# A decoder layer's front: feature-major rows, two native first chunks, the row scale entering at their sums

## The chip, the cores and the metric

The kernel runs on one core of one Trainium2 chip, in one launch. The metric is the time of the core in device microseconds (us); lower is better. Engines are named as in the profile: PE (TensorE matmul), PEld (its weight load), DVE (VectorE), ACT (ScalarE), POOL (GpSimd), SP (SyncE, which here only issues DMAs).

## The reference, cut to what matters

One layer of a hybrid decoder over 256 positions of width 1,024, in float32:

```
n = RMSNorm(x) * norm_mix_g
z = n @ w_in              # c_a, c_g, q, k, v, qi, ki, wi, gate logits
u = c_a * sigmoid(c_g)    # 1024 channels
u = causal depthwise conv of u, 31 taps, + conv_b
y_conv = silu(LayerNorm(u)) @ w_conv_out
y_attn = DSA(q, k, v, qi, ki, wi) @ w_attn_out       # top 64 of the keys by an index score
h = x + (g_conv * y_conv + g_attn * y_attn) @ w_mix_out
h = h + CrossAttn(RMSNorm(h), RMSNorm(mem))          # 256 memory rows
h = h + relu(RMSNorm(h) @ w_ff1)^2 @ w_ff2
out = RMSNorm(h)
```

RMSNorm divides a row by the root of its mean square, so the divisor (here `rstd`, one number for each of the 256 positions) is a factor of the whole row, while the gain `norm_mix_g` belongs to the 1,024 features. A product with the weights can therefore be taken before the row's factor is known, and the factor put to the result.

## The kernel before

**Layout and stream.** Activations lie feature-major: 8 tiles (`kt`) of 128 features by 256 positions. All weights come through one stream of chunks (`STREAM`, L34 to L53), in the order in which PE uses them: four `conv` chunks, `qi`, `ki`, four more `conv`, `gc`, `ga`, `v`, `q` and `k`, `xk`, `xv`, `ao`, `co`, `mix` and so on. A chunk is 1 MB, [128 x 2,048] float32, and holds two output tiles ("halves") of 8 `kt` each. For `conv` the first half is the gate, the second the value. Three buffers (`raws`) hold the raw chunks; a few (`EARLY`) lie elsewhere. `load` issues the DMA of the next chunk from SP, and is called when a chunk's last half has been split.

**Two ways to multiply.** Ordinarily each half of weights is split into a high part (ACT, L178) and a low part (DVE, the `lo` of L181), both in the form fp32r, and so are the activations (`n2`). A tile is then three products for each `kt`, 24 matmuls (`tile_b`). A chunk in `WHOLE` is instead multiplied in native float32, unsplit: 8 matmuls for a tile, each of which the profile lists as two records. Before, `conv` 0 and `co` 0 are in `WHOLE`.

**The front (L321 to L410).** Two DMAs bring x row-major (`x_rm`). ACT squares and sums each row (`row_square`), DVE and POOL make `rstd`, DVE scales the rows, PE transposes them, ACT and DVE take them out of PSUM times the gain (`n_f`), then split them into `n2`. Ten matmuls of zeros (`ps_warm`) run ahead on PE. `vec`, the gains and biases, comes by a DMA that POOL issues (L325).

**The convolution.** `conv_in` (L471) makes `u` of one channel tile. Its 31 taps run one instruction each: the first on ACT, the other 30 on DVE, as jobs in a list `fill`. When all eight tiles have had their taps, `layer_norm` (L595) is started as a generator. Its steps go one at each call of `tick`: reserve a tile; mean on PE (`ps_mub`), subtraction, squares, sums; the last sums (`vs`); the square root (`ps_vr`, POOL's power `rs_vr`); the spread (`ps_rsb`), the product with it and Silu on `acc`, after which `normed` is set; then the split of `acc` into `u2` in four steps. Ahead of the `co` chunks the program drains `fill` and calls `tick` until `normed` is set (L705 to L708). `co` 0 multiplies `acc` itself in native float32; `co` 1 to 3 use `u2`.

**Who goes when.** The program is written in one order, by hand, and each engine executes its part of it in order. What DVE does between PE's tiles is dealt out while the program is written, by a planner with prices of its own, which are numbers in the code and not measurements. `pe.total` grows by 2,560 for a tile of 24 matmuls. `dve.total` grows by elements / 0.96 + 70 (125 with a scalar from a pointer): 1,137 for a `lo`, 337 for a product of 256, 391 down to 360 for a tap as its length falls from 255 to 226. `tick`, called after each tile, steps the generators and then hands out taps:

```
        while (len(fill) > 1 or (fill and (len(done) > 5 or nused[0] < 5))) and dve.total < pe.total - 1000:
            fill_one()
        dve.total = max(dve.total, pe.total - 2000)
```

Each use of weights also calls `split_ahead` (L213), which puts one `lo` on DVE and one high part on ACT for halves that come later. Both totals are set to zero at the end of the front (L410).

Of the kernel before, what the change touches and what calls it, by code (L numbers as in the profile page):

```python
# [8 lines left out]
F32 = mybir.dt.float32  # L9
# [3 lines left out]
ALU = mybir.AluOpType  # L13
# [42 lines left out]
N_CHUNK = KT * S  # L56
HALVES = 6
EARLY = (3, STREAM.index(("co", 0)))
WHOLE = (("conv", 0), ("co", 0))


class Counted:
# [49 lines left out]
def block_kernel(ctx, tc, x, xt, mem, memt, wst, wki, vecs, convw, gout, out):  # L112
# [30 lines left out]
    def ps_acc(name):  # L143
        return bank("acc", 4, name)
# [9 lines left out]
    def load(parts=1):  # L154
        if nload[0] >= len(STREAM):
            return
        c = nload[0]
        nload[0] += 1
        key = STREAM[c]
        raw = t8(f"raw{c}", F32, (P, N_CHUNK)) if c in EARLY else raws.tile([P, N_CHUNK], F32, tag="raw", name=f"raw{c}")  # L160
        n = KT * NK if key[0] == "ki" else N_CHUNK
        src = wki if key[0] == "ki" else wst[INDEX[key]]
        for q in range(parts):
            ns = slice(q * n // parts, (q + 1) * n // parts)
            nc.sync.dma_start(raw[:, ns], src[:, ns])
        if key in WHOLE:
            whole[key] = raw.rearrange("p (k n) -> p k n", k=2 * KT)
            return
        parts = 1 if key[0] == "ki" else 2
        for q in range(parts):  # L170
            ns = slice(q * n // parts, (q + 1) * n // parts)
            high_jobs.append(lambda ns=ns, q=q, last=q == parts - 1: high(key, c, raw, ns, q, last))
# [82 lines left out]
    def tile_b(ps, w, x2, kts=range(KT), wide=False):  # L255


        ps = ps[: w[0].shape[2]]
        for kt in kts:
            wh, wl = w[0][:, kt, :], w[1][:, kt, :]  # L260
            if not wide:
                mm_b(ps[:, :S], wh, wl, x2, kt, kt == 0, kt == KT - 1)
            elif kt == 0:
                pe.matmul(ps, wh, x2.both(kt), start=True, stop=False)
                pe.matmul(ps[:, S:], wl, x2.high(kt), start=False, stop=False)
            else:
                pe.matmul(ps[:, S:], wl, x2.high(kt), start=False, stop=False)
                pe.matmul(ps, wh, x2.both(kt), start=False, stop=kt == KT - 1)
# [49 lines left out]
        return lambda ct, ps: act(dst[:, ct, :], ps, AF.Copy)  # L318


    x_rm = t8("x_rm", F32, (P, 2, D))  # L321
    for rb in range(2):
        nc.sync.dma_start(x_rm[:, rb, :], x[rb * P : (rb + 1) * P, :])
    vec = cst.tile([P, 72], F32, name="vec")
    nc.gpsimd.dma_start(vec, vecs)  # L325
    bgc, bga, cvb, lng, lnb, g_mix, g_mem, g_x, g_ffn = (vec[:, 8 * j : 8 * j + 8] for j in range(9))
    cw = cst.tile([P, KT, TAPS], F32, name="cw")
    for parts in (2, 2, 1):
        load(parts)
    nc.sync.dma_start(cw, convw.rearrange("p (k t) -> p k t", k=KT))  # L330
    load()
    zero = w2("zero")
    nc.vector.memset(zero, 0.0)
# [12 lines left out]
    nc.scalar.activation(half, half, AF.Sigmoid, bias=0.0, scale=0.0)  # L346
    nc.gpsimd.memset(half, -0.5)
    ps = ps_aux("ps_warm")
    for j in range(10):
        nc.tensor.matmul(ps, zero_r[:, :P], zero_r, start=True, stop=True)  # L350


# [5 lines left out]
    def row_square(src, rb, ss):  # L358
        junk = w2(f"junk_{src.name if hasattr(src, 'name') else ''}{rb}", BF16, (P, D))
        act(junk, src[:, rb, :], AF.Square, accum_out=ss[:, rb : rb + 1])  # L360

    def rsqrt(sums, name):

        ps = ps_aux(f"ps_{name}")
        for rb in range(2):
            pe.matmul(ps[:, 2 * rb : 2 * rb + 2], sums[:, rb * P : rb * P + P], onesd[:, :2], start=True, stop=True)
        ms = small.tile([P, 2], F32, tag="ms", name=f"ms_{name}")
        dve.tensor_scalar(ms, ps[:, :4].rearrange("p (r t) -> p r t", r=2)[:, :, 0], EPS, None, ALU.add)
        return power(ms, name)
# [12 lines left out]


    n2 = parts_t8("n_p")
    n_f = t8("n_f")
    ss = small.tile([P, 2], F32, tag="ss", name="ss_n")
    ptn = [ps_acc(f"pt_n{c}") for c in range(4)]
    for rb in range(2):
        row_square(x_rm, rb, ss)
    for rb in range(2):  # L390
        ms = small.tile([P, 1], F32, tag="ms1", name=f"ms_n{rb}")
        dve.tensor_scalar(ms, ss[:, rb : rb + 1], 1.0 / D, EPS, ALU.mult, ALU.add)
        rs = small.tile([P, 1], F32, tag="rs1", name=f"rs_n{rb}")
        nc.gpsimd.tensor_tensor(out=rs, in0=ms, in1=half[:, 0:1], op=ALU.pow)
        dve.tensor_scalar(x_rm[:, rb, :], x_rm[:, rb, :], rs[:, 0:1], None, ALU.mult)
        for kt in range(KT):
            pe.transpose(ptn[kt // 2][:, (kt % 2) * S + rb * P : (kt % 2) * S + rb * P + P],
                         x_rm[:, rb, kt * P : kt * P + P], ident)
    for kt in range(KT):
        src = ptn[kt // 2][:, (kt % 2) * S : (kt % 2) * S + S]  # L400
        if kt % 2 == 1:
            dve.tensor_scalar(n_f[:, kt, :], src, g_mix[:, kt : kt + 1], None, ALU.mult)
        else:
            act(n_f[:, kt, :], src, AF.Copy, scale=g_mix[:, kt : kt + 1])
    for c in range(0, KT, 2):
        split(n2.high(c, 2), n2.low(c, 2), n_f[:, c : c + 2, :])
    split_high()
    split_low()
    split_high()
    pe.total = dve.total = 0.0  # L410


    mem2 = parts_t8("mem_p")
# [3 lines left out]
    def memory():  # L417
        mem_rm = t8("mem_rm", F32, (P, 2, D))
        mem_t = t8("mem_t")
        nc.sync.dma_start(mem_rm, mem.rearrange("(r p) d -> p r d", p=P))  # L420
        nc.sync.dma_start(mem_t, memt)
        yield
        yield
        yield
        ss = small.tile([P, 2], F32, tag="ss", name="ss_m")
        for rb in range(2):
            row_square(mem_rm, rb, ss)
            yield
        dve.tensor_scalar(ss, ss, 1.0 / D, EPS, ALU.mult, ALU.add)
        nc.gpsimd.tensor_tensor(out=rs_m, in0=ss, in1=half, op=ALU.pow)  # L430
# [26 lines left out]
        return go  # L457

    def conv_tile(i, half):
        key = ("conv", i)  # L460
        w = weights("conv", i, half, KT) if key not in WHOLE else None
        split_ahead()
        ps = ps_mm(f"ps_conv{i}{half}")
        if w:
            tile_b(ps, w, n2)
        else:
            for kt in range(KT):
                pe.matmul(ps[:, :S], whole[key][:, half * KT + kt, :], n_f[:, kt, :], start=kt == 0, stop=kt == KT - 1)
        return ps

    def conv_in(i):  # L471
        psg = conv_tile(i, 0)
        sg = w2(f"sg{i}", F32, (P, S))
        act(sg, psg[:, :S], AF.Sigmoid)
        tick()
        psa = conv_tile(i, 1)
        dve.tensor_tensor(out=u[:, i, :], in0=psa[:, :S], in1=sg, op=ALU.mult)
        tick()
        tap(i, 0)()
        fill.append([tap(i, s) for s in range(1, TAPS)])  # L480
        if ("conv", i) in WHOLE:
            load()

    for i in range(4):
        conv_in(i)
        if i == 1:
            start(memory())


    qi_t = t8("qi_t", F32, (P, 4, S))  # L490
# [635 lines left out]
```

## Time and profile before

| | |
|---|---|
| median of 3 runs | 516.89 us (516.72 to 516.94) |
| the profiled execution: its own time | 516.86 us |
| its span, first to last instruction | 515.1 us |
| mean granted TensorE clock | 0.998 |
| busy: PE, PEld, DVE, ACT, POOL | 98%, 90%, 81%, 56%, 4% |
| DMA | 92.75 MB, mean 180 GB/s |

The span is 1.76 us shorter than the execution's own time; that remainder is taken as fixed. PE's busy share says that the matmuls follow each other, not that each is as fast as it could be. In a timeline row the two numbers ahead are the start and the length of a merged group, `xN` is its count of instructions, and the brackets hold the idle time ahead of it and who ended it.

### The profile page before, as it was taken

Reading aid. Unit: us, or ns where it says so; the run is one execution under the profiler, and the core shown is the slowest. Engines: PE = TensorE matmul, PEld = TensorE weight load, DVE = VectorE, ACT = ScalarE, POOL = GpSimd, SP = SyncE. Lnnn points to the kernel's source line nnn. Section 1 sums busy time; section 2 is a strip of 40 time slices with the busy share of each in tenths; the row PEclk is TensorE's granted clock in tenths of the full one; section 3 lists DMA queues with packets and bytes.
Section 4 is the critical chain, followed back from the end, with each engine's and each line's share of the span. In section 5 each row is a group of like instructions: output and inputs, shape, how many; then the busy total and the mean of one; then the engine's idle time right before and its main releaser. Section 6 shows DMA issues by size and latency. Waiting matters only on the chain.

```text
span 515.1 us, 8515 instructions
## 1 busy us (share of the span) xinstructions
PE 504.3 (98%) x3354; PEld 463.1 (90%) x3354; DVE 419.4 (81%) x796; ACT 286.9 (56%) x489; POOL 19.2 (4%) x30
## 2 busy tenths in 40 slices
PE   7999999999999999999999999999999999999995
PEld 5999999999899999999999998988888888888884
DVE  4998999999988999999898976696766566666565
ACT  5666655546446666656655657565654454554442
POOL 2000000001001000021000000000000000000000
PEclk9999999999999999999999999999999999999999
DMA  8856435464552343454744541446445554445402
GB/s 317 359 187 236 155 122 205 174 225 183 194 216 102 144 164 118 155 224 161 275 143 155 207 184 44 181 165 242 164 169 220 221 207 163 164 174 219 181 1 81
DMA packets 14311, 92.75 MB, mean 180 GB/s; under 512 B 1584, under 2 KB 2480, under 8 KB 3776
## 3 DMA queue, kind: packets, MB, share of 16 engines
q1 hardware_dynamic: 13952, 91.85, 48.3%
q8 instruction: 26, 0.43, 0.3%
q10 hardware_dynamic: 288, 0.33, 0.2%
q14 instruction: 13, 0.11, 0.1%
q0 software_dynamic: 32, 0.04, 0.0%
HBM read 91.16 MB, written 1.05 MB: 179 GB/s over the span
## 4 chain that ended last, share of the span: by engine, by line
PE 95%; issue 1%; ACT 1%; DVE 1%; DMA 1%; POOL 0%; POOLq 0%; DVEq 0%; ACTq 0%
PE ps_f L77 17%; PE ps_ff L77 16%; PE ps_conv L77 9%; PE ps_co L77 5%; PE ps_ao L77 4%; PE ps_ga L77 4%; PE ps_gc L77 4%; PE ps_k L77 4%; PE ps_q L77 4%; PE ps_mix L77 4%; PE ps_v L77 4%; PE ps_xo L77 3%; PE ps_xq L77 2%; PE ps_qi L77 2%; PE ps_xk L77 2%; PE ps_xv L77 2%
## 5 line engine op out<-in xcount | busy, mean ns | idle before, releaser
L77 DVE TENSOR_TENSOR lo<-raw,hi 128x1024 fp32r<-128x1024 f32 x161 | 195.7, 1225 | 3.3 <-ACT hi L178 1.6
L178 ACT ACTIVATE hi<-raw 128x1024 fp32r<-128x1024 f32 x161 | 166.4, 1047 | 2.5 <-PE ps_v L77 2.5
L77 DVE SCALAR_TENSOR_TENSOR acc<-u,cw,acc 128x255 f32<-128x255 f32 (+27 forms) x240 | 100.6, 475 | 0.6
L77 PE MATMUL ps_f<-ff_p,hi 128*128 128x512 f32 x256 | 89.8, 396 | 0.0
L77 PE MATMUL ps_ff<-hi,fs 128*128 128x512 f32 (+1 forms) x256 | 80.8, 387 | 0.0
L77 PE MATMUL ps_f<-ff_p,lo 128*128 128x256 f32 x256 | 66.2, 279 | 0.0
L77 PEld LDWEIGHTS ps_ff<-hi,fs 128*128 128x128 f32 x256 | 47.9, 188 | 9.2
L77 PEld LDWEIGHTS ps_f<-ff_p,hi 128*128 128x128 f32 x256 | 46.8, 188 | 9.2
L77 DVE TENSOR_TENSOR ft<-ps_f,ft 128x256 f32<-128x256 f32 x32 | 13.6, 423 | 46.4 <-ACT ft L957 46.4
L77 PEld LDWEIGHTS ps_f<-ff_p,lo 128*128 128x128 f32 x256 | 48.2, 188 | 2.6
L957 ACT ACTIVATE ft<-ps_f 128x256 f32<-128x256 f32 x32 | 12.2, 380 | 66.9 <-PE ps_f L77 66.9
L77 PE MATMUL ps_ff<-lo,fs 128*128 128x512 f32 (+1 forms) x128 | 49.4, 386 | 0.0
L77 PE MATMUL ps_conv<-n_p,hi 128*128 128x256 f32 x224 | 41.0, 285 | 0.0
L77 PEld LDWEIGHTS ps_conv<-n_p,hi 128*128 128x128 f32 x224 | 34.9, 192 | 0.8 <-issue 0.7
L77 PE MATMUL ps_conv<-n_p,lo 128*128 128x256 f32 x112 | 31.7, 283 | 0.0
L77 PEld LDWEIGHTS ps_ff<-lo,fs 128*128 128x128 f32 x128 | 24.1, 188 | 4.9
L77 PE MATMUL ps_q<-n_p,hi 128*128 128x256 f32 x128 | 24.4, 291 | 0.0
L77 PE MATMUL ps_ao<-o_p,hi 128*128 128x256 f32 x128 | 23.5, 285 | 0.0
L77 PE MATMUL ps_k<-n_p,hi 128*128 128x256 f32 x128 | 23.4, 284 | 0.0
L77 PE MATMUL ps_gc<-n_p,hi 128*128 128x256 f32 x128 | 23.1, 283 | 0.0
L77 PE MATMUL ps_ga<-n_p,hi 128*128 128x256 f32 x128 | 23.1, 283 | 0.0
L77 PE MATMUL ps_mix<-mix_p,hi 128*128 128x512 f32 (+1 forms) x80 | 22.1, 350 | 0.0
(229 smaller groups left out, 1003.3 us busy)
## 6 DMA issues: line engine op xcount, KB each, us to landing
raw<-in_wst_dram SPq DMA_DIRECT2D x80, 1024.0 KB, 4.8
raw<-in_wst_dram SPq DMA_DIRECT2D x4, 512.0 KB, 7.7
x_rm<-in_x_dram SPq DMA_DIRECT2D x2, 512.0 KB, 3.9
mem_rm<-in_mem_dram SPq DMA_DIRECT2D x1, 1024.0 KB, 9.0
mem_t<-in_memt_dram SPq DMA_DIRECT2D x1, 1024.0 KB, 11.0
h_t<-in_xt_dram SPq DMA_DIRECT2D x1, 1024.0 KB, 6.9
out_dram<-hg SPq DMA_DIRECT2D x4, 176.0 KB, 2.2
g_out<-in_gout_dram SPq DMA_DIRECT2D x1, 512.0 KB, 7.0
```

The lines of the kernel that those rows point to most:

```text
L77: return fn(*args, **kwargs)
L178: act(hi, raw[:, ns], AF.Copy)
L957: act(t, ps[:, S:], AF.Copy)
```

## The change

x is no longer loaded row-major and transposed. Its feature-major copy (`xt`), which before is read only for the residual, is loaded in two DMAs with rows of 4 KB, the second of them between the two halves of the first chunk. `conv` 1 joins `WHOLE`. The gain alone is put to x (`xg`), and `conv` 0 and 1 are multiplied natively from `xg`; `rstd` is made beside them from squares on ACT, sums on DVE, a matmul with ones, POOL's power and a spread over the partitions (`rsb`), in a generator `row_scale` whose steps stand among PE's matmuls. From `rsb` come `n2` for everything later, and the sums of the first two chunks are multiplied by it, gate and value. Six `ps_warm` matmuls are left of ten. At the end of this new front `pe.total` is set to 0 and `dve.total` to 2,000, before `conv` 2; the memory's loads start there too.

```
-WHOLE = (("conv", 0), ("co", 0))
+WHOLE = (("conv", 0), ("conv", 1), ("co", 0))
...
             nc.sync.dma_start(raw[:, ns], src[:, ns])
+            if c == 0 and q == 0:
+                nc.sync.dma_start(x_t[:, 4:8, :], xt[:, 4:8, :])
...
-    x_rm = t8("x_rm", F32, (P, 2, D))
-    for rb in range(2):
-        nc.sync.dma_start(x_rm[:, rb, :], x[rb * P : (rb + 1) * P, :])
+    x_t = t8("x_t")
...
-    for parts in (2, 2, 1):
+    nc.sync.dma_start(x_t[:, 0:4, :], xt[:, 0:4, :])
+    for parts in (2, 1):
         load(parts)
     nc.sync.dma_start(cw, convw.rearrange("p (k t) -> p k t", k=KT))
+    load()
     load()
...
-    for j in range(10):
+    for j in range(6):
         nc.tensor.matmul(ps, zero_r[:, :P], zero_r, start=True, stop=True)
...
+    for kt in range(KT):
+        gain(kt, None if kt in (0, 2) else dve)
+    for hf in range(2):
+        act(n_f[:, 4 * hf : 4 * hf + 4, :], x_t[:, 4 * hf : 4 * hf + 4, :], AF.Square)
+    for n in (4, 2, 1):
+        dve.tensor_tensor(out=n_f[:, :n, :], in0=n_f[:, :n, :], in1=n_f[:, n : 2 * n, :], op=ALU.add)
+
+    def row_scale():
+
+        rs = rsqrt(n_f[:, 0, :], "n")
+        yield
+        act(rsb, spread(rs, "rsb_n"), AF.Copy)
+        yield
+        for c in range(0, KT + 2, 2):
+            if c < KT:
+                dve.tensor_tensor(out=n_f[:, c : c + 2, :], in0=xg[:, c : c + 2, :],
+                                  in1=rsb.unsqueeze(1).to_broadcast([P, 2, S]), op=ALU.mult)
+                act(n2.high(c, 2), n_f[:, c : c + 2, :], AF.Copy)
+            if c > 0:
+                dve.tensor_tensor(out=n2.low(c - 2, 2), in0=n_f[:, c - 2 : c, :], in1=n2.high(c - 2, 2).bitcast(F32),
+                                  op=ALU.subtract)
+            if c == 2:
+                split_high()
+            if c == 4:
+                split_low()
+        split_high()
+        split_low()
+        split_high()
+        yield
...
-    for i in range(4):
+    def conv_in_first():
+
+        scaling, banks = row_scale(), []
+        for i in range(2):
+            for half in range(2):
+                ps = ps_acc(f"ps_conv{i}{half}")[:, :S]
+                banks.append(ps)
+                for kt in range(KT):
+                    pe.matmul(ps, whole[("conv", i)][:, half * KT + kt, :], xg[:, kt, :], start=kt == 0,
+                              stop=kt == KT - 1)
+                    if kt == KT // 2 - 1 and i == 0 and half == 1:
+                        next(scaling)
+                if half == 1:
+                    load()
+                if i == 0 and half == 1:
+                    next(scaling)
+                    next(scaling)
+        for i in range(2):
+            psg, psa = banks[2 * i : 2 * i + 2]
+            sg = w2(f"sg{i}", F32, (P, S))
+            dve.tensor_tensor(out=sg, in0=psg, in1=rsb, op=ALU.mult)
+            act(sg, sg, AF.Sigmoid)
+            dve.tensor_tensor(out=sg, in0=sg, in1=rsb, op=ALU.mult)
+            gated_linear(i, psa, sg)
+
+    conv_in_first()
+    split_low()
+    pe.total = 0.0
+    dve.total = 2000.0
+    start(memory())
+    for i in range(2, 4):
         conv_in(i)
-        if i == 1:
-            start(memory())
```

`gated_linear` is the second half of the old `conv_in`: u = value times gate on DVE, then `tick` unless the chunk is in `WHOLE`, tap 0 on ACT, and the other 30 taps into `fill`. `conv_tile` loses its native branch.

More of the change, by code (lines that the diff above doesn't have):

```diff
@@ L384, in block_kernel @@
     n2 = parts_t8("n_p")
+    xg = t8("xg")
     n_f = t8("n_f")
[L386 to L398, printed above, removed]
@@ L399, in block_kernel @@
-    for kt in range(KT):
[L400 to L410, printed above, removed]
+    rsb = w2("rsb", F32, (P, S))
@@ new lines, in gain @@
+    def gain(kt, engine):
+        if engine is dve:
+            dve.tensor_scalar(xg[:, kt, :], x_t[:, kt, :], g_mix[:, kt : kt + 1], None, ALU.mult)
+        else:
+            act(xg[:, kt, :], x_t[:, kt, :], AF.Copy, scale=g_mix[:, kt : kt + 1])
+    for kt in range(KT):
+        gain(kt, None if kt in (0, 2) else dve)
[3 more added lines that the diff above has]
+        dve.tensor_tensor(out=n_f[:, :n, :], in0=n_f[:, :n, :], in1=n_f[:, n : 2 * n, :], op=ALU.add)
@@ L459, in conv_tile @@
     def conv_tile(i, half):
-        key = ("conv", i)
-        w = weights("conv", i, half, KT) if key not in WHOLE else None
+        w = weights("conv", i, half, KT)
         split_ahead()
         ps = ps_mm(f"ps_conv{i}{half}")
[L464 to L468, printed above, removed]
+        tile_b(ps, w, n2)
         return ps
@@ L476, in conv_in, with gated_linear @@
         psa = conv_tile(i, 1)
-        dve.tensor_tensor(out=u[:, i, :], in0=psa[:, :S], in1=sg, op=ALU.mult)
-        tick()
+        gated_linear(i, psa[:, :S], sg)
+    def gated_linear(i, ps, sg):
+        dve.tensor_tensor(out=u[:, i, :], in0=ps, in1=sg, op=ALU.mult)
+        if ("conv", i) not in WHOLE:
+            tick()
         tap(i, 0)()
         fill.append([tap(i, s) for s in range(1, TAPS)])
-        if ("conv", i) in WHOLE:
-            load()
-    for i in range(4):
+    def conv_in_first():
[27 more added lines that the diff above has]
+    for i in range(2, 4):
         conv_in(i)
-        if i == 1:
-            start(memory())
     qi_t = t8("qi_t", F32, (P, 4, S))
```

## The prediction

> **What bounds the kernel now.** I read the page first, then PE's waits, then the timelines of the two places that the change reaches: the front and, because of the planner, the end of the taps.
>
> ```profile
> span 515.1 us, 8515 instructions
> PE 504.3 (98%) x3354; PEld 463.1 (90%) x3354; DVE 419.4 (81%) x796; ACT 286.9 (56%) x489; POOL 19.2 (4%) x30
> ...
> PE 95%; issue 1%; ACT 1%; DVE 1%; DMA 1%; POOL 0%; POOLq 0%; DVEq 0%; ACTq 0%
> ```
>
> ```profile
> PE ps_warm L350 <- DVE zero_r L335: 1.9, 1, 1.9
> PE pt_n L77 <- DVE ms_n L77: 1.3, 1, 1.3
> PE ps_xo L77 <- ACT xptr L853: 0.8, 1, 0.8
> PE pt_n L77 <- DVE x_rm L77: 0.4, 1, 0.4
> ```
>
> These four are all of PE's waits: between the transposes and the end PE stands still once, for 0.8 us. So whatever moves PE's first real matmul, adds matmuls, or opens a hole later, moves the end by as much. The change must be summed on PE alone, and DVE, at 81%, matters where PE comes to wait for it. Two places follow.
>
> **The front: when PE may start, and what it must do.**
>
> ```profile
> 0.74 0.86 SPq L323 DMA_DIRECT2D x_rm<-in_x_dram  x2
> 1.24 0.75 POOL L325 DMA_DIRECT2D vec<-in_vecs_dram  x1 [0.79 <-POOLq L1117]
> 4.27 1.06 ACT L360 ACTIVATE junk_x_rm<-x_rm 128x1024 bf16<-128x1024 f32 x1 [1.42 <-DMA x_rm<-in_x_dram]
> 9.12 1.57 ACT L404 ACTIVATE n_f<-pt_n,vec 128x256 f32<-128x256 f32 x4 [2.43 <-PE pt_n L77]
> 9.65 7.26 PE L77 MATMUL ps_conv<-n_f,raw 128*128 128x256 f32 x32
> 16.56 0.58 PE L77 MATMUL ps_conv<-n_p,hi 128*128 128x256 f32 x2
> ```
>
> ```profile
> L77 PE MATMUL ps_conv<-n_p,lo x16: 278/283/283, 17.0 to 22.4; 128*128 128x256 f32 x16
> L380 ACT ACTIVATE mem_p<-mem_t,vec x8: 493/500/510, 43.4 to 66.2; 128x256 fp32r<-128x256 f32 x8
> ```
>
> ```profile
> x_rm<-in_x_dram SPq DMA_DIRECT2D x2, 512.0 KB, 3.9
> ...
> vec<-in_vecs_dram POOLq DMA_DIRECT2D x1, 36.0 KB, 5.5
> ```
>
> Before, PE starts `conv` 0 at 9.65; it takes 6.91 us natively (to 16.56), `conv` 1 takes 5.9 split, and `conv` 2 starts at 22.5. The first half of x lands at 4.27, when its square starts; the second DMA of that size, whose place the first weights take, at about 5.5 (issued 0.4 later, and the median of the two is 3.9 to landing). But every gain needs `vec`, issued at 1.24 and landed 5.5 us later, at 6.74. Before, nothing needed it until 9.12. Now the first `xg` tile comes at 6.74 plus 0.50 (an ACT scaling of that size, L380): PE starts at 7.3, 2.35 us earlier. The transposes go, and with them their waits; that gain is already in the 2.35.
>
> The Trainium skill's page "DMA: Bandwidth & Descriptors", section "Anatomy of one DMA", fits a DMA issued by POOL at 2.0 us plus its bytes over 436 GB/s, which would be an estimate of 2.1 us for `vec`; the first weights would then bind at 5.5, and the sum would be some 1.7 us lower. The row says 5.5 us, and I go by it.
>
> From 7.3 PE does two native chunks, 2 x 6.91 = 13.8 us, where it did 6.91 + 5.9: this costs 1.0 us. Beside them it executes two small steps, root and spread, of the kind seen further down at 242.83 and 246.14: about 0.4 and 0.3 us. With 0.2 us for the change of form (the first rows of `conv` 1 are that much slow), `conv` 2 starts at 22.0: a gain of 0.5 us. That holds if DVE keeps up. Squares: two gains and two squares on ACT to 6.74 + 1.0 + 2.1 = 9.8; sums on DVE 1.2 + 0.6 + 0.4, so 12.1, and PE asks for them after twelve calls, 7.3 + 12 x 0.43 = 12.5. Power and spread end at 15.4. Then DVE has four products and four subtractions of 0.63 us and two `lo` of 1.22 (rows below), to 22.9, of which only the last `lo` is needed later than 22.0, at 24.9. The six products for the gates at 0.42, two sigmoid waits of 0.4 and the next `lo` end near 27.5, and `conv` 3 asks at 27.8. All of it is covered, by 0.3 us at the tightest place; without the cover each tenth is lost one for one, so I allow 0 to 1 us above.
>
> **The taps: what the planner no longer hands out early.** `tick` gives DVE taps as long as `dve.total` is 1,000 below `pe.total`. Before, the ticks of `conv` 0 to 3 gave 0, 0, 7, 3, 3, 3, 4, 3 taps, 23 in all, which the trace confirms:
>
> ```profile
> L77 DVE SCALAR_TENSOR_TENSOR acc<-u,cw,acc x23: 464/480/490, 18.6 to 35.5; 128x255 f32<-128x255 f32 x3, 128x254 f32<-128x254 f32 x3, 128x253 f32<-128x253 f32 x3, 128x252 f32<-128x252 f32 x3
> ```
>
> ```profile
> 227.31 1.95 DVE L77 SCALAR_TENSOR_TENSOR acc<-u,cw,acc 128x235 f32<-128x235 f32 x4
> 229.17 1.22 DVE L77 TENSOR_TENSOR lo<-raw,hi 128x1024 fp32r<-128x1024 f32 x1
> 230.31 1.94 DVE L77 SCALAR_TENSOR_TENSOR acc<-u,cw,acc 128x231 f32<-128x231 f32 x4
> 232.16 1.22 DVE L77 TENSOR_TENSOR lo<-raw,hi 128x1024 fp32r<-128x1024 f32 x1
> 233.30 0.94 DVE L77 SCALAR_TENSOR_TENSOR acc<-u,cw,acc 128x227 f32<-128x227 f32 x2
> 234.15 2.90 DVE L77 TENSOR_TENSOR lo<-raw,hi 128x1024 fp32r<-128x1024 f32 x2
> ```
>
> After, counting starts at `conv` 2 with `dve.total` at 2,000. Tick 1: 2,000 against 2,560 - 1,000, no tap. Tick 2: 2,000 + 1,137 + 337 = 3,474 against 4,120, two taps. Ticks 3 and 4 give four and three. That is 9, and both planners then stand 650 below `pe.total`: the new one has handed out 14 fewer taps and has no credit to show for it. From there each tick has the same prices, and the old planner always had taps waiting, so no idle DVE time can absorb the 14. They arrive in `ao`, whose ticks leave 2,560 - 1,137 = 1,423, about four taps (the rows: 4, 4 and the last 2). Carrying the sums through all ticks: after `ao` tile 1 the old planner has 2 left, the new one 17 at -946; tile 2 leaves 13, tile 3 leaves 9, tile 4 leaves 5, tile 5 leaves 1 at -731, and tile 6 takes it. Before, the last tap was handed out after tile 2. The layer norm starts four tiles late. There is one `lo` less in stock too: the one ending at 233.38 serves the tile that starts behind the mean at 236.9, 3.5 us of cover, from which a tile's 2.88 us goes; it just holds.
>
> **What four tiles cost.**
>
> ```profile
> 236.65 0.59 PE L77 MATMUL ps_mub<-usum,onesd 128*128 128x256 f32 x2
> 237.28 1.88 DVE L77 TENSOR_TENSOR acc<-acc,ps_mub 128x512 f32<-128x512 f32 x3 [0.23 <-PE ps_mub L77]
> 241.99 0.42 DVE L77 TENSOR_TENSOR vs<-vs 128x256 f32<-128x256 f32 x1
> 242.83 0.50 PE L77 MATMUL ps_vr<-onesd,vs 128*128 128x2 f32 x4
> 243.46 0.15 DVE L77 TENSOR_SCALAR ms_vr<-ps_vr 128x2 f32<-128x2 f32 x1
> 243.70 1.61 POOL L355 TENSOR_TENSOR rs_vr<-ms_vr,half 128x2 f32<-128x2 f32 x1 [7.73 <-DVE ms_vr L77]
> 246.14 0.38 PE L77 MATMUL ps_rsb<-ident,rs_vr 128*128 128x128 f32 x2
> 246.56 2.48 DVE L77 TENSOR_TENSOR acc<-acc,ps_rsb 128x512 f32<-128x512 f32 x4 [1.81 <-PE ps_rsb L77]
> 248.13 4.03 ACT L625 ACTIVATE acc<-acc,vec 128x256 f32<-128x256 f32 x8
> 249.23 2.97 PE L77 MATMUL ps_co<-acc,raw 128*128 128x256 f32 x13
> 39.14 0.85 POOL L430 TENSOR_TENSOR rs_m<-ss_m,half 128x2 f32<-128x2 f32 x1 [31.34 <-DVE ss_m L77]
> ```
>
> Before, the mean is taken behind tile 4, the root behind 6, the spread behind 7, and tile 8 covers the first Silu: 12.6 us from mean to `co` 0, all under PE's tiles. After, the tick of tile 7 reserves, that of tile 8 takes the mean, and the rest is drained with PE waiting. Its length: mean to the last sum 236.65 to 242.41, 5.76; root and its DVE step 0.83; POOL's power 0.85 plus 0.1 (the 1.61 ran beside a DVE `lo`, which is not there now; the two are the ends); spread 0.42; the first product 0.68; the first Silu 0.59; handovers 0.1: 9.3. Later Silus come every 0.5, faster than `co` 0 takes them. PE's own 0.7 in these steps was paid before too: 8.6 us net. In `co` 0 DVE then has the four `u2` steps and three `lo` that it had before; they end about when asked.
>
> ```profile
> L350 PE MATMUL ps_warm<-zero_r x10: 389/628/796, 1.9 to 5.4; 128*128 128x512 f32 x10
> ```
>
> ```profile
> 508.00:509.00 1.00, 0.76 (x7) 0.55 (x5) 0.97 (x3) 0.51 (x2) 0.00 (x0) 1.00 0.31 111
> ...
> 513.00:514.00 1.00, 0.00 (x0) 0.00 (x0) 0.00 (x0) 0.00 (x0) 0.00 (x0) 0.72 0.41 149
> 514.00:515.00 1.00, 0.00 (x0) 0.00 (x0) 0.00 (x0) 0.00 (x0) 0.00 (x0) 0.50 0.00 0
> ```
>
> Such a hole may also cost clock. At the end PE stops at 508.76 and the granted clock (third number from the right) falls to 0.50 within 513 to 514, 4.7 us later; the 1.3 us waits of the front left it at 1.00. The new hole has 5.4 us without a matmul and then two short ones. At the start, the median of ten matmuls took 628 ns and the fastest 389, so those at half speed fill some 3 us, which loses 1.5. I take 1.5, with 0 and 3 as ends. The Trainium skill, "TensorE: Matmul & The Clock Gate", Part 1, says that an idle window of about 3.4 us halves the clock and a busy one restores it; the rows agree in direction, and by that rule, an estimate, the loss is 1.7 to 3.4 us and the sum 526.7 to 528.4.
>
> **Sum.** Against the profiled execution's 516.86, which stands 0.03 below the median: -0.5 + 8.6 + 1.5 = +9.6, so 526.5. About 1 us (0.2%) is what a measurement of this kernel can tell from no change.
>
> **Rivals.** *The front is all that counts* (the other side). If the taps are in time, only the 0.5 us remains, 516.4, and if `vec`, with x in other pieces beside it, lands when the first weights do, at 5.5, another 1.2 goes: 515.2. It decides at two taps: the tick of tile 2 had room for two more, and a norm one tile late already shows 1.7 us of spread, product and Silu. For it speaks that DVE has 19% free; against it, that the planner hands out no taps on DVE's real idle time. 0.05 for faster, 0.03 for no change. *One tile less late*: the one leftover tap fits after tile 5; a 2.88 us tile covers the mean, and the hole is too short for the clock: 516.4 + 5.8 + 0.5 = 522.7. 0.10. *The clock holds*: the two short matmuls keep it up, 525.0. 0.18. *A front at half clock*: six warming matmuls end near 4.6, and 2.7 us of idle follow; if PE then starts at half speed it loses 1.5 to 2 more, 528.3. For it speaks that the old front had at most 1.3 us idle; against it, that six at half speed already fill nearly the 3 us in which the clock rose. 0.12.
>
> **Numbers.** The forecast has 0.52. The range 523.0 to 529.0 holds it with its clock bounds, the clock that holds and the front at half clock; it leaves out the first rival, most of the second, and the tails. Slower by over 0.2% is all but the first rival: 0.92.
>
> **What the changed profile would show.** `vec` landing near 6.7 with the first gain behind it; 64 native `ps_conv` records from 7.3 to 21; `conv` 2 near 22.0; nine taps where there were 23; the last tap behind `ao` tile 6; `ps_mub` behind the last `ps_ao`; PE's waits led by `ps_vr` for DVE `vs`, near 5 us, then `ps_rsb` and `ps_co`, over 1 us each; the clock below 1 near 257. A mean still behind tile 4, or no such waits, would prove me wrong.

## The result, and the profile after

| | before | after |
|---|---|---|
| median (range) | 516.83 us (516.72 to 516.94) | 531.80 us (531.62 to 532.47) |
| ratio, 95% interval | | 1.0292 [1.0277, 1.0307] |
| the profiled execution | 516.86 us, span 515.1 | 531.62 us, span 529.8 |
| mean granted clock | 0.998 | 0.989 |

The change costs 15.0 us where 9.6 were forecast, and lies above the range. The page of after, its lines on the span, the engines, the chain that ended last and the clock:

```profile
span 529.8 us, 8453 instructions
PE 508.1 (96%) x3324; PEld 464.6 (88%) x3324; DVE 421.5 (80%) x804; ACT 284.8 (54%) x484; POOL 18.3 (3%) x29
...
PEclk9999999999999999999699999999999999999999
...
PE 91%; DVE 3%; ACT 2%; issue 1%; DMA 1%; POOL 0%; POOLq 0%; DVEq 0%; ACTq 0%
```

One slice of the clock's line has fallen to 6. All of PE's waits in after (who waited, for what: us in total, times, longest):

```profile
PE ps_vr L77 <- DVE vs L77: 5.3, 1, 5.3
PE ps_conv L77 <- ACT xg L395: 3.7, 1, 3.7
PE ps_warm L352 <- DVE zero_r L337: 1.9, 1, 1.9
PE ps_co L77 <- ACT acc L666: 1.5, 1, 1.5
PE ps_conv L77 <- ACT sg L485: 1.3, 1, 1.3
PE ps_rsb L77 <- POOL rs_vr L357: 1.0, 1, 1.0
PE ps_xo L77 <- ACT xptr L894: 0.8, 1, 0.8
```

Three of these, 5.3 and 1.0 and 1.5, are the layer norm's steps in a row, as forecast. The 3.7 lies ahead of the first product; the 1.9 and the 0.8 are in before too. The 1.3 for `sg` was not forecast. Where the two traces stand apart, by the first matmul of a stage:

| starts at, us | before | after | after minus before |
|---|---|---|---|
| first product | 9.65 | 8.53 | -1.12 |
| `conv` 2 | 22.49 | 25.03 | +2.54 |
| `qi` | 34.01 | 38.29 | +4.28 |
| `ao` | 225.13 | 229.41 | +4.28 |
| `co` 0 | 249.23 | 262.54 | +13.31 |
| `mix` | 273.40 | 288.21 | +14.81 |

So 4.3 us are lost before `qi`, nothing in the next 190 us, 9.0 between `ao` and `co`, and 1.5 in `co`. Each of the three places is read in its own timeline.

**The front.** Its timeline in after:

```profile
1.25 0.74 POOL L325 DMA_DIRECT2D vec<-in_vecs_dram  x1 [0.80 <-POOLq L1158]
1.92 2.93 PE L352 MATMUL ps_warm<-zero_r 128*128 128x512 f32 x6 [1.92 <-DVE zero_r L337]
7.97 0.91 ACT L395 ACTIVATE xg<-x_t,vec 128x256 f32<-128x256 f32 x2 [5.12 <-DMA vec<-in_vecs_dram]
8.53 7.54 PE L77 MATMUL ps_conv<-xg,raw 128*128 128x256 f32 x24 [3.68 <-ACT xg L395]
```

`vec` lands at 7.95, not 6.74. The issues of the front's DMAs (the last number is us from issue to landing) give the first weights 6.6 us from their issue at 1.17, so 7.78, not 5.5:

```profile
raw<-in_wst_dram SPq DMA_DIRECT2D x1, 512.0 KB, 6.6
vec<-in_vecs_dram POOLq DMA_DIRECT2D x1, 36.0 KB, 6.7
```

The records of `conv` 0 and 1, in two stretches (count, ns shortest/median/longest, first to last start):

```profile
L77 PE MATMUL ps_conv<-xg,raw x10: 521/634/797, 8.5 to 12.5; 128*128 128x256 f32 x10
L77 PE MATMUL ps_conv<-xg,raw x54: 379/379/521, 12.5 to 24.8; 128*128 128x256 f32 x54
```

All 64 records are there (the one at 12.5 stands in both rows, and the last starts at 25.00). But ten of them fill 8.53 to 12.81, 0.43 us each, and the others follow each other every 0.22: the first 4.3 us ran at half clock, which costs ten times 0.21, 2.1 us. The windows' clock column is no help here; it gives 1.00 until the trace's first clock event, and that event is a rise at 12.81. The lengths of the records tell it.

**The 1.3 us at `conv` 3.** ACT and PE around it in after:

```profile
30.56 0.60 ACT L462 ACTIVATE acc<-u,vec,cw 128x256 f32<-128x256 f32 x1 [1.02 <-DVE u L77]
31.07 1.04 ACT L180 ACTIVATE hi<-raw 128x1024 fp32r<-128x1024 f32 x1
32.02 0.36 ACT L485 ACTIVATE sg<-ps_conv 128x256 f32<-128x256 f32 x1
32.43 0.51 PE L77 MATMUL ps_conv<-n_p,hi 128*128 128x256 f32 x2 [1.30 <-ACT sg L485]
```

PE needs the PSUM bank that holds the gate of `conv` 2. That gate waits to be read by the Sigmoid of L485, and ACT does its work in order: ahead of it stand tap 0 of channel tile 1 (30.56), which in turn waited 1.02 us for `u` from DVE, and a high part of weights (31.07). So a bank that was full and ready kept PE out.

**Between `ao` and `co`.** First the taps up to 40 us as a group, then the last of them and the norm's steps on PE:

```profile
L77 DVE SCALAR_TENSOR_TENSOR acc<-u,cw,acc x9: 472/475/477, 33.6 to 39.7; 128x255 f32<-128x255 f32 x3, 128x254 f32<-128x254 f32 x3, 128x253 f32<-128x253 f32 x3
```

```profile
248.50 0.45 DVE L77 SCALAR_TENSOR_TENSOR acc<-u,cw,acc 128x226 f32<-128x226 f32 x1
252.45 0.59 PE L77 MATMUL ps_mub<-usum,onesd 128*128 128x256 f32 x2
258.36 0.99 PE L77 MATMUL ps_vr<-onesd,vs 128*128 128x2 f32 x4 [5.31 <-DVE vs L77]
260.37 0.69 PE L77 MATMUL ps_rsb<-ident,rs_vr 128*128 128x128 f32 x2 [1.03 <-POOL rs_vr L357]
262.54 3.82 PE L77 MATMUL ps_co<-acc,raw 128*128 128x256 f32 x10 [1.47 <-ACT acc L666]
```

Nine taps where there were 23, the last one alone at 248.50, the mean behind the last `ao` tile, and then PE standing still: the chain that the prediction wrote down, step by step. The windows around it (the number ahead of the last two is the granted clock):

```profile
254.00:255.00 1.00, 0.00 (x0) 0.00 (x0) 0.96 (x2) 1.00 (x3) 0.00 (x0) 1.00 1.08 459
255.00:256.00 1.00, 0.00 (x0) 0.00 (x0) 0.94 (x2) 0.62 (x2) 0.00 (x0) 0.58 1.01 426
...
264.00:265.00 1.00, 1.00 (x4) 0.82 (x3) 1.00 (x2) 1.00 (x3) 0.00 (x0) 0.50 0.00 0
265.00:266.00 1.00, 1.00 (x6) 0.83 (x5) 0.96 (x3) 1.00 (x3) 0.00 (x0) 0.80 0.00 0
```

The clock falls at 255.16, in the hole, and returns at 265.40, when `co` 0 has run for almost 3 us. From `co` to `mix` after takes 25.67 us instead of 24.17.

### The profile page after: what moved, and what is told of

It reads as the page before. It is cut to its first block, busy times and chain, and to the rows that moved or that the text cites. A ratio compares the mean times of both kernels' runs of the same rounds, so it can differ in the third digit from the quotient of the medians.

```text
span 529.8 us, 8453 instructions
## 1 busy us (share of the span) xinstructions
PE 508.1 (96%) x3324; PEld 464.6 (88%) x3324; DVE 421.5 (80%) x804; ACT 284.8 (54%) x484; POOL 18.3 (3%) x29
## 4 chain that ended last, share of the span: by engine, by line
PE 91%; DVE 3%; ACT 2%; issue 1%; DMA 1%; POOL 0%; POOLq 0%; DVEq 0%; ACTq 0%
PE ps_f L77 17%; PE ps_ff L77 16%; PE ps_conv L77 7%; PE ps_co L77 5%; PE ps_ga L77 4%; PE ps_gc L77 4%; PE ps_ao L77 4%; PE ps_k L77 4%; PE ps_q L77 4%; PE ps_mix L77 4%; PE ps_v L77 4%; PE ps_xo L77 3%; PE ps_xq L77 2%; PE ps_qi L77 2%; PE ps_xk L77 2%; PE ps_xv L77 2%
## 5 line engine op out<-in xcount | busy, mean ns | idle before, releaser
L77 DVE TENSOR_TENSOR lo<-raw,hi 128x1024 fp32r<-128x1024 f32 x159 | 192.4, 1219 | 4.7 <-ACT hi L180 3.2
L180 ACT ACTIVATE hi<-raw 128x1024 fp32r<-128x1024 f32 x159 | 164.0, 1047 | 0.0
L77 DVE SCALAR_TENSOR_TENSOR acc<-u,cw,acc 128x241 f32<-128x241 f32 (+27 forms) x240 | 100.0, 469 | 0.5
L77 PE MATMUL ps_conv<-n_p,hi 128*128 128x256 f32 x192 | 35.4, 286 | 1.3 <-ACT sg L485 1.3
L77 PEld LDWEIGHTS ps_conv<-n_p,hi 128*128 128x128 f32 x192 | 29.9, 191 | 2.3 <-ACT sg L485 1.5
L77 PE MATMUL ps_conv<-n_p,lo 128*128 128x256 f32 x96 | 27.1, 283 | 0.0
```

The source lines that it names most:

```text
L77: return fn(*args, **kwargs)
L180: act(hi, raw[:, ns], AF.Copy)
```

## Experiments

My theory at this point: the 9.0 and the 1.5 come from the planner alone (14 taps no longer handed out early), and the 4.3 from the front, in three parts: late DMAs, a cold clock, the bank. The rival for the first: the hole comes from the front's own lateness, which pushes DVE's work back until the taps are late. The rivals for the front: one cause, `vec`, makes all of it; or the DMAs as a whole.

**The planner alone.** The kernel before, with its old front, is given fewer taps to hand out.

```
-    pe.total = dve.total = 0.0
+    pe.total, dve.total = 0.0, 7600.0
```

> The kernel before, with one number changed: at the end of its front dve.total starts at 7,600 in place of 0, so that the planner hands out 9 taps by the end of conv 3 instead of 23, as the changed kernel does. Front, DMAs and arithmetic stay. Theory (the planner's lost credit makes the layer norm late): last tap behind ao tile 6, ps_mub behind the last ps_ao, PE waits near 5.3 us for vs, 1.0 for rs_vr and 1.5 for acc, net 9.0 us, and 1.5 us of clock: 527.3 us. Rival (the late layer norm comes from the new front's own lateness, or DVE catches up in its idle time): within 1 us of 516.8.

Measured: 528.87 us (527.79 to 529.01), 1.0227 [1.0212, 1.0242]. The groups and PE's timeline of this kernel:

```profile
L77 DVE SCALAR_TENSOR_TENSOR acc<-u,cw,acc x9: 474/476/478, 28.7 to 35.3; 128x255 f32<-128x255 f32 x3, 128x254 f32<-128x254 f32 x3, 128x253 f32<-128x253 f32 x3
```

```profile
248.02 0.59 PE L77 MATMUL ps_mub<-usum,onesd 128*128 128x256 f32 x2
253.92 0.99 PE L77 MATMUL ps_vr<-onesd,vs 128*128 128x2 f32 x4 [5.31 <-DVE vs L77]
255.94 0.69 PE L77 MATMUL ps_rsb<-ident,rs_vr 128*128 128x128 f32 x2 [1.03 <-POOL rs_vr L355]
258.10 2.50 PE L77 MATMUL ps_co<-acc,raw 128*128 128x256 f32 x5 [1.47 <-ACT acc L625]
```

Nine taps again, the same three waits to the hundredth, `co` 0 8.9 us later than before (258.10 against 249.23), and 2.05 us lost from there to `mix` at half clock (251.84 to 262.08). None of the front's work was touched: from `ao` to `co` this kernel takes 33.12 us, as after does, where before takes 24.10. The one number that the planner starts from accounts for all of the hole; the rival falls.

**The new front with credit.** To after is added what gives the taps back: the planner's DVE total is lowered in `ga` and `v`, long before `ao`.

```
+            if kind == "ga":
+                dve.total -= 340.0
...
+            if kind == "v":
+                dve.total -= 340.0
```

> The changed kernel, and the 14 taps given back late: each of the 8 tiles of ga and the 8 steps of v lowers dve.total by 340, 5,440 in all. Nothing else. Theory (only the planner's sums withheld the taps, DVE has the time): last tap handed out behind ao tile 2, no wait of PE at the layer norm, 531.8 - 9.0 - 1.5 = 521.3 us. Rival (DVE is too full, the taps push the low parts of the weights): PE waits of 1 to 4 us for lo in v, q, k or ao, 522 to 525 us.

Measured: 522.12 us (521.70 to 522.48), 1.0101 [1.0086, 1.0116]. PE's waits for the norm are gone from its list, and the mean is back inside `ao`:

```profile
241.15 0.59 PE L77 MATMUL ps_mub<-usum,onesd 128*128 128x256 f32 x2
247.33 0.50 PE L77 MATMUL ps_vr<-onesd,vs 128*128 128x2 f32 x4
```

That takes back 9.7 of the 15.0 us; `qi` still starts 3.9 late, and some 1.3 more are lost on the way to `mix` (`ao` +4.5, `co` +4.7, `mix` +5.2). Of these, 0.45 fall in `v`, where the low parts come just late behind the taps; 0.5 fall in `co` at 266, where PE waits for DVE's `gc_t`. The rest is the front.

**The cold clock.** 24 warming matmuls instead of six.

```
-    for j in range(6):
+    for j in range(24):
```

> The changed kernel with 24 matmuls of zeros in place of 6, so that PE is kept busy up to the first real matmul at 8.5 us. Theory (six leave the clock at half until 12.8 us): the first ten conv records come 0.22 us apart in place of 0.43, conv 2 starts 2.1 us earlier, 529.7 us; somewhat less if that uncovers DVE behind it. Rival (the first products are paced by weights landing, or by xg, not by the clock): 531.8, records still 0.43 apart.

Measured: 531.22 us (530.16 to 532.03), 1.0279 [1.0260, 1.0297]. PE's timeline and the records to 12.8 us:

```profile
1.92 7.48 PE L352 MATMUL ps_warm<-zero_r 128*128 128x512 f32 x24 [1.92 <-DVE zero_r L337]
9.24 5.34 PE L77 MATMUL ps_conv<-xg,raw 128*128 128x256 f32 x24
```

```profile
L77 PE MATMUL ps_conv<-xg,raw x17: 378/379/379, 9.2 to 12.7; 128*128 128x256 f32 x17
```

The clock rises at 5.64 and holds: the first product starts 0.7 later, because the zeros fill PE, and `conv` 2 starts 1.5 earlier (23.53). Together that is 2.2, the 2.1 of the ten slow records: shown. `qi` and the first `co` keep the 1.5 (36.8 and 261.0), but the half clock in `co` then costs 2.1 instead of 1.5 in this trace, so the profiled execution gains 0.9 and the median 0.6. Over the seven kernels with the hole this loss was 1.5 to 2.9 us (after, and the one with x in 8 KB rows below), and in each it is about half the time from `co` 0's first matmul to the clock's return: 2.9 us in after, 5.6 in that one.

Where the return comes, the traces tell. In each of the fourteen, the clock's changes lie whole multiples of 3.413 us apart (in after 71, 3 and 77 of them). Counted in such steps from these changes, the clock rose behind every step in which PE, as the trace models it, was busy for 84% or more, and behind none with 78% or less; it fell behind every one with 44% or less and behind none with 47% or more. One step of after with its six zeros, and one of before (its stretch, its length, PE's busy time):

```profile
2.57:5.98 3.41, 2.28 (x6) 1.28 (x4) 0.00 (x0) 0.20 (x1) 0.32 (x4) 1.00 0.86 227
1.44:4.85 3.41, 2.93 (x7) 2.35 (x8) 0.42 (x1) 1.36 (x3) 1.37 (x7) 1.00 0.90 309
```

Behind the first (67%) the clock stayed low; behind the second (86%) it rose, though by then PE had been busy only as long as six zeros keep it. Where the steps lie against the program's start differs from one execution to the next, so the loss in the hole and the fate of a few zeros differ with it.

**`vec` alone.** `vec` is issued first, by SP.

```
-    nc.gpsimd.dma_start(vec, vecs)
+    nc.sync.dma_start(vec, vecs)
```

> The changed kernel with the DMA of vec issued first on SP in place of POOL. Theory (vec alone holds the first gain; x and the first weights are there by 5.6): vec lands before 5 us, PE's first product at about 6.0 in place of 8.5, conv 2 2.5 us earlier, about 529.3 us, with the same half clock at its start or a shorter one (528.5). Rival (x or the weights land only near 8 too): 531 to 531.8.

Measured: 532.34 us (530.66 to 532.50), 1.0291 [1.0275, 1.0308]. The DMAs, and PE's wait:

```profile
vec<-in_vecs_dram SPq DMA_DIRECT2D x1, 36.0 KB, 1.9
raw<-in_wst_dram SPq DMA_DIRECT2D x1, 512.0 KB, 6.8
```

```profile
PE ps_conv L77 <- DMA raw<-in_wst_dram: 3.8, 1, 3.8
```

`vec` needs 1.9 us instead of 6.7 and is there at 2.6, and nothing is gained: the first product starts at 8.62, and PE now waits for the first weights, which land at 8.48. The trace of after names ACT's `xg`, and so `vec`, because that came last; but the weights had come only 0.2 us before it, and here they come later still, 0.46 of it because `vec` now stands ahead of them in SP's issues (1.63 against 1.17).

**The bank.** Both early gates' Sigmoids are put ahead of the taps, so that ACT comes sooner to `conv` 2's.

```
-        for i in range(2):
-            psg, psa = banks[2 * i : 2 * i + 2]
-            sg = w2(f"sg{i}", F32, (P, S))
-            dve.tensor_tensor(out=sg, in0=psg, in1=rsb, op=ALU.mult)
+        sgs = [w2(f"sg{i}", F32, (P, S)) for i in range(2)]
+        for i, sg in enumerate(sgs):
+            dve.tensor_tensor(out=sg, in0=banks[2 * i], in1=rsb, op=ALU.mult)
             act(sg, sg, AF.Sigmoid)
+        for i, sg in enumerate(sgs):
             dve.tensor_tensor(out=sg, in0=sg, in1=rsb, op=ALU.mult)
-            gated_linear(i, psa, sg)
+        for i, sg in enumerate(sgs):
+            gated_linear(i, banks[2 * i + 1], sg)
```

> The changed kernel with the tail of its first two chunks reordered: both gate sums scaled and both sigmoids first, then both products with the row scale, then both values; in the changed kernel chunk 1 follows chunk 0. Theory (PE's 1.3 us wait at conv 3 is a PSUM bank that the sigmoid of conv 2 has not read yet, because ACT holds it behind tap 0 of chunk 1, which waits for DVE): that sigmoid moves from 32.0 to about 31.0, the wait falls to 0.3 us, 530.8 us. Rival (ACT is held by the high parts of the weights, or PE by the low parts on DVE): the wait stays above 1 us, 531.8.

Measured: 530.81 us (530.41 to 532.16), 1.0270 [1.0255, 1.0286]. ACT's timeline:

```profile
27.09 0.76 ACT L517 ACTIVATE sg<-sg 128x256 f32<-128x256 f32 x2 [0.68 <-DVE sg L77]
28.67 1.09 ACT L462 ACTIVATE acc<-u,vec,cw 128x256 f32<-128x256 f32 x2 [0.83 <-DVE u L77]
30.62 0.36 ACT L485 ACTIVATE sg<-ps_conv 128x256 f32<-128x256 f32 x1
```

The gate of `conv` 2 is read at 30.62 instead of 32.02, the 1.3 us wait is not among PE's any more, and `qi` starts 1.4 earlier (36.88). The cause is shown. PE still starts `conv` 3 right behind that Sigmoid (30.98 to 31.03), some 0.2 us late, too little for the list of waits. The median gains only 1.0; in the trace the half clock then cost 2.1 in `co` (261.1 to 287.4).

**Why the first DMAs are late: three looks.** With `vec` out of the way, is it x in two pieces that holds the weights up? Here x comes in one DMA of 8 KB rows, ahead of the weights (on top of the `vec` edit).

```
-                nc.sync.dma_start(x_t[:, 4:8, :], xt[:, 4:8, :])
...
-    nc.sync.dma_start(x_t[:, 0:4, :], xt[:, 0:4, :])
+    nc.sync.dma_start(x_t, xt)
```

> The changed kernel with vec first on SP (as in e4) and x_t in one DMA with rows of 8 KB ahead of the first weights, in place of two with rows of 4 KB around them. Theory (the first 2.5 MB or so come at half rate up to about 6.5 us whatever their shape): x lands near 6.5 to 7, the first weights near 8 to 8.5, PE's first product at 8.5 as in e4, 532 us. Rival (the two pieces with 4 KB out of every 8 KB are what is slow, as x in whole rows came at full rate before): x at 5.5, weights at 7, first product at 7.1, about 530.8 us.

Measured: 531.76 us (530.82 to 532.38), 1.0281 [1.0264, 1.0298]. All of x, 1 MB, is there at 6.08, when its first half alone came at 5.84 in the kernel with only the `vec` edit; the weights' first half still takes 2.05 us more, to 8.13.

Next, the first half of the first chunk goes ahead of x (on top of the `vec` edit).

```
+                nc.sync.dma_start(x_t[:, 0:4, :], xt[:, 0:4, :])
                 nc.sync.dma_start(x_t[:, 4:8, :], xt[:, 4:8, :])
...
-    nc.sync.dma_start(x_t[:, 0:4, :], xt[:, 0:4, :])
```

> The changed kernel with vec first on SP (as in e4), and the first half chunk of weights issued ahead of both pieces of x. Theory A (each of the two tensors is slow at its first half megabyte, some 2.6 us in place of 1.3): weights land near 5.8, x near 8.5, second piece of x and later DMAs at 1.3 us each, first product near 9, 532 us or a little more. Theory B (only the weight tensor is slow at first, x never): weights near 5.8, x at 7.1, first product at 7.7, about 531.3 us.

Measured: 532.76 us (532.07 to 533.61), 1.0304 [1.0289, 1.0319]. Weights at 5.98, first half of x at 8.37, its second at 9.66. Whichever comes second is 2.4 to 2.6 us behind the first (here, and in the kernel with only the `vec` edit), so the order is not the cause; the first half MB of each tensor is slow and the other half takes 1.3. That fits two theories: that anything early is slow, or that pieces which take 4 KB out of every 8 KB row are slow as long as the other half has not been read.

**Everything mended.** After with the credit, the gates together, 16 warming matmuls and `vec` issued by ACT.

```
+            if kind == "ga":
+                dve.total -= 340.0
...
-    nc.gpsimd.dma_start(vec, vecs)
+    nc.scalar.dma_start(vec, vecs)
...
-    for j in range(6):
+    for j in range(16):
...
```

> The changed kernel with four things mended at once: vec issued from ACT, 16 warming matmuls, the gates together (e5), the 14 taps given back in ga and v (e2). From e2's 522.1: clock about 1.5 to 2.1 less, gates 1.0 less, first product at 7.9 in place of 8.3, 0.4 less: about 518.9 us, still above the 516.8 of before, since the second native chunk (1.1 us) and the root and spread on PE (0.6 us) eat what the earlier start (1.7 us) gives, and DVE has nothing to spare. Rival (the parts do not add: DVE is the bound once the layer norm is in time, so an earlier PE only waits for low parts): 520.5 to 522.

Measured: 518.57 us (518.25 to 518.75), 1.0030 [1.0019, 1.0041]. Of the 15.0 us 13.2 are back, as the sum of the parts had it. `qi` starts at 34.5, 0.5 behind before, and `mix` 1.8 behind it; the first product, at 8.17, still waits for the weights.

**Pieces in one stretch.** The same, with the two halves of x and of the first chunk lying in arrays of their own, so that each DMA reads 512 KB without gaps, and 12 warming matmuls.

```
-            nc.sync.dma_start(raw[:, ns], src[:, ns])
+            nc.sync.dma_start(raw[:, ns], src[:, ns] if c else w0[q])
...
-                nc.sync.dma_start(x_t[:, 4:8, :], xt[:, 4:8, :])
+                nc.sync.dma_start(x_t[:, 4:8, :], x[1])
...
-    nc.sync.dma_start(x_t[:, 0:4, :], xt[:, 0:4, :])
+    nc.sync.dma_start(x_t[:, 0:4, :], x[0])
```

> e8 with the two pieces of x and the two halves of the first chunk read from arrays of their own, each 512 KB in one stretch of memory, where e8 reads 4 KB out of every 8 KB; 12 warming matmuls in place of 16, so that PE is free by about 6.5. Theory (the strided reads make the first pieces slow, as the row-major x of the kernel before, 512 KB in one stretch, came at 1.3 us a piece): first piece of x at 4.3, weights at 5.6 to 6.7, first product at 6.7, conv 2 1.4 us earlier, 517.2 us, about even with before. Rival (the first pieces are slow whatever their stretch, about 200 GB/s up to 6.5 us): weights at 8, first product at 8.2, 518.6 us as e8.

Measured: 517.40 us (516.63 to 517.94), 1.0001 [0.9993, 1.0010]. The DMAs, issued at 0.74, 1.18 and 1.64, and PE:

```profile
x_t<-in_x_dram SPq DMA_DIRECT2D x1, 512.0 KB, 3.7
raw<-in_w_dram SPq DMA_DIRECT2D x1, 512.0 KB, 4.5
x_t<-in_x_dram SPq DMA_DIRECT2D x1, 512.0 KB, 5.4
```

```profile
7.20 5.69 PE L77 MATMUL ps_conv<-xg,raw 128*128 128x256 f32 x24
```

The four pieces land at 4.43, 5.72, 7.01 and 8.28, one every 1.28 us from the first on. So early DMAs aren't slow as such; the strided ones were: in the kernel just before, x was there at 5.89 and the weights at 8.04, 2.15 apart. By what mechanism, and why the other halves of the same rows then run at the full rate, no run shows. The weights are there at 5.72, but PE is busy with zeros until 7.20.

**How many zeros.** Eight warming matmuls instead of twelve.

```
-    for j in range(12):
+    for j in range(8):
```

> e9 with 8 warming matmuls in place of 12, nothing else: in e9 they held PE until 7.2 us, though x had landed at 4.4 and the weights at 5.7. Theory (products at half clock are still products): first product at 5.8, at half clock until the clock rises near 6 to 8, so 0.7 to 1.4 us earlier at conv 2; 516.2 to 516.9 us where e9 gave 517.4 (516.9 beside it). Rival (DVE, which has nothing to spare in v and q, takes it back there): 517.2.

Measured: 516.85 us (516.27 to 519.15, two of twelve runs above 519), 1.0008 [0.9998, 1.0018]: no difference from before. The same solid pieces land 0.7 us later in this trace (x at 5.11, weights at 6.39, still 1.28 apart), so the first product starts at 6.53 and not at 5.8. `conv` 2 starts at 20.90 and `qi` 1.2 us ahead of before, but at `ao` only 0.6 is left and at `mix` nothing (273.5). Of the 1.3 lost on the way 0.45 go in `v`, as in the first kernel with credit, and 0.5 in `co`, for `gc_t`.

**Spread credit, eight and ten zeros.** The same credit is spread over `ga`, `v`, `q` and `k`; then the same with ten.

```
-            if kind == "ga":
-                dve.total -= 340.0
+            if kind in ("ga", "q", "k"):
+                dve.total -= 340.0 if kind == "ga" else 85.0
...
-                dve.total -= 340.0
+                dve.total -= 170.0
```

> e10 with the 14 taps given back more evenly: 340 a tile in ga, 170 a step in v, 85 a tile in q and k; the last tap still behind ao tile 2. Theory (the low parts arrive just late in v and early q because taps crowd there): from conv 2 to ao the 0.6 us that e9 lost against the kernel before come back, 515.7 to 516.4 us, a little below before. Rival (DVE's total is the bound, wherever the taps go): as e10.

> e11 with 10 warming matmuls in place of 8. e11's times lie in two groups, 515.7 to 516.4 and 518.1 to 518.8. Theory (eight at 0.43 us end at 5.3 and leave 1.2 us idle ahead of the first product, and in half of the runs the clock had then not risen; the two more close that gap): the upper group goes, times 515.7 to 517.0, median 516.3, about 0.1% below before. Rival (the groups come from elsewhere): two groups again.

With eight: 517.22 us (515.73 to 518.78), 1.0008 [0.9996, 1.0020], in two groups, 515.7 to 516.4 and 518.1 to 518.8. With ten: 516.34 us (515.99 to 516.73), 0.9986 [0.9977, 0.9995], and the upper group does not appear in 11 runs. Two more zeros removed the upper group, which would fit a clock that rises in time or doesn't: with eight, PE is idle for 0.94 us ahead of the first product (5.54 to 6.48), and a step of 3.41 us that holds this whole gap is only 73% busy, an estimate from that trace. But the trace is of a run in the lower group (516.28), and the runs of before beside the kernel with ten lie in two groups as well (516.6 to 517.1 and 517.4 to 517.9), so this stays open. PE's waits with ten, apart from the 1.9 us for the zeros, and its front:

```profile
PE ps_xo L77 <- ACT xptr L899: 0.8, 1, 0.8
PE ps_co L77 <- DVE gc_t L77: 0.2, 1, 0.2
```

```profile
1.91 4.63 PE L354 MATMUL ps_warm<-zero_r 128*128 128x512 f32 x10 [1.91 <-DVE zero_r L339]
6.34 5.63 PE L77 MATMUL ps_conv<-xg,raw 128*128 128x256 f32 x24
```

This is the only version whose interval lies below before, by 0.14%, which is under the 0.2% named in the prediction. PE starts 3.3 us earlier than before, and 0.5 to 0.7 of it reaches the end. The loss in `v` is gone with the spread (`q` starts 1.1 us ahead of before, as `qi` does); that in `co` is not. There DVE has five low parts between the norm's last product and its first `gc_t`, where it had four before, and `co` takes 24.68 us instead of 24.17. That fits the one `lo` less in stock, of which the prediction said that it just holds; no run puts the `lo` back.

## Why the prediction was right or wrong

**Right: the hole.** The steps of "The taps" and "What four tiles cost" held as written: nine taps, the last behind `ao` tile 6, `ps_mub` behind the last `ps_ao`, waits near 5, over 1 and over 1 (5.3, 1.0, 1.5), 8.6 us forecast and 9.0 measured; the old front with the same starting number gives 9.0 from `ao` to `co` too. From the mean to `co` 0 it took 10.1 us where 9.3 were worked out, because the root's and the spread's matmuls met the half clock too: 0.99 and 0.69 us instead of 0.50 and 0.38, which is the 0.8. Net it is only 0.4 more, because PE's own steps, priced at 0.7, took 1.1 in before.

**Right: the clock in the hole.** 1.5 us were taken, between 0 and 3; 1.5 came in after, 2.05 with the old front. That it was just 1.5 was luck: the seven kernels with the hole lost 1.5 to 2.9, by where the hole fell on the steps of 3.41 us. The case that the clock holds is out. In after the fall came 2.7 us after the mean's two matmuls began (252.45 to 255.16), and in all seven it came ahead of `ps_vr`, so the short `ps_vr` and `ps_rsb` came too late to keep the clock up; it stayed low for 10.24 us. By the rule that the prediction quoted from the Trainium skill, "TensorE: Matmul & The Clock Gate", Part 1, the loss would have been an estimated 1.7 to 3.4 us; the 1.5 to 2.9 of the traces overlap that and lie a little lower.

**Wrong: when the front's first product can start.** The step that failed is "the second DMA of that size, whose place the first weights take, at about 5.5", and beside it `vec` "at 6.74". The place in the queue was right and the piece was not: before, the second DMA was the second half of x by rows, one solid stretch; now it is half of a chunk whose rows alternate with its other half. These landed at 7.78, and `vec`, which shares the engines with them, at 7.95. The start came at 8.53 instead of 7.3: 1.2 us. Where `vec` was early, PE started 0.14 behind the weights' landing (8.48 to 8.62), so by an estimate the weights make half of the 1.2 and `vec` with its gain the other half. The row that would have told it was in the trace of before and I did not read it. The first half chunk, issued there at 1.65:

```profile
raw<-in_wst_dram SPq DMA_DIRECT2D x1, 512.0 KB, 6.5
```

So it landed at 8.11, 2.6 us behind the half of x ahead of it (5.52), while the two solid pieces of x followed each other in 1.27.

**Wrong: the front at half clock.** This was a rival with 0.12, priced at 1.5 to 2 more; it happened, at 2.1. The argument against it, "six at half speed already fill nearly the 3 us in which the clock rose", failed, because it took one trace's rise for the rule. In before the clock rose 2.9 us after the first zero, at 4.85; other traces, with no gap on PE up to the rise, show 4.2 (the old front with fewer taps, at 6.08) and 5.0 (ten zeros, at 6.93). With six it never rose before real products had run for 2.9 us or more, in any of the six profiles. The argument also counted on a start at 7.3; at 8.53 the idle time was 3.7 us, not 2.7.

**Wrong: "All of it is covered, by 0.3 us at the tightest place".** I followed what DVE owes PE and left out what ACT owes it: the bank of `conv` 2's gate, read by an ACT that works in order behind tap 0 and a high part. 1.3 us. With that wait gone, `conv` 2 to `qi` still takes 11.9 us against 11.5. Half of the 0.4 is the change from native to split products, which in before lies ahead of `conv` 2 and which the prediction had in its 22.0; the other half is `conv` 3's start, still behind the Sigmoid.

The sum by its terms: the front -0.5 forecast, +4.3 measured; the hole 8.6 and 9.0; the clock 1.5 and 1.5. The miss lies in the front: 1.2 for the start, 2.1 for the clock and 1.3 and 0.2 for the bank make the 4.8 between -0.5 and +4.3. The credit, the gates together, 16 zeros and `vec` by ACT gave 13.2 of the 15.0 us back in one kernel, with the weights still as late (8.04); the pieces in one stretch, with 12 zeros, gave another 1.2.

## What to carry to other kernels

A planner's starting number is part of the schedule: a reset moved by two chunks took 14 small steps from DVE's early idle time, and PE paid for them 200 us later, with a layer norm four tiles late and a clock that fell. Price a DMA by the row of that very tensor and shape, not by its place in the queue, and ask what lands next when the latest is made early: 5 us off `vec` gained nothing. For each PSUM bank that PE wants back, write down who reads it last and what stands ahead of that instruction on its engine.

## What was not expected of the hardware

- Half-megabyte pieces that read 4 KB of each 8 KB row landed 2.05 to 3.3 us behind the piece ahead of them when they were the first of their tensor (3.3 in the old front with fewer taps, 8.64 behind 5.37); the same bytes in one stretch took 1.28, and the second halves of the same rows 1.3 to 1.6.
- A DMA of 36 KB took 4.7 to 6.7 us when POOL issued it beside the big ones, and 1.9 when SP issued it first.
- The clock changed only at steps of 3.413 us. A step with PE busy for 84% or more raised it, 78% did not; 44% or less lowered it, 47% did not. These are the nearest cases of fourteen traces, not measured thresholds. So six warming matmuls of zeros, busy from 1.92 to 4.85, left the clock low in all six kernels with six, while eight had it up at 5.25 and 6.11.
- Once lost in the hole, the clock stayed at half for 10.24 us, three steps, in all seven kernels with the hole, although PE was at `co` 0 again after 4.7 to 7.4.
